# State-space heads: a select in place of four subtractions, one product for M, and an output projection cut into halves and quarters

## The chip, the cores and the metric

The kernel runs on one core of a Trainium2 chip, as one launch. The metric is device time in microseconds (us). Engines are named as in the profile: PE is TensorE (PEld its weight load), DVE is VectorE, ACT is ScalarE, POOL is GpSimd, SP issues most DMAs.

## The reference, cut to what matters

Six stages follow each other: a Mamba-2 mixer, three convolutional feed-forward blocks, a differential attention and a sparse-attention block. The change is in the first, the mixer, on 256 positions, 32 heads of 64 channels, two chunks of 128 positions:

```python
zxbcdt = rms_norm(x, ln_g) @ in_w                 # z, xs, B, C, dt
xbc = silu(causal_dwconv(xbc, conv_w, conv_b))
dt = softplus(dt + dt_bias); a = dt * (-exp(a_log))
a_cs = cumsum(a) within a chunk                   # per head
decay_in = exp(where(l >= s, a_cs[l] - a_cs[s], -inf))
y_diag = einsum('bcgls,bgrcls,bcsgrp->bclgrp', C B^T, decay_in, xs * dt)
y_off  = (state that enters chunk 1) read by C, times exp(a_cs)
y = (y_diag + y_off + xs * d_skip) * silu(z)
y = rms_norm(y in 4 groups of 512 channels) * norm_g
x = x + y @ out_w                                 # 2048 -> 1024
```

With two chunks, everything between source and target positions is three blocks of 128 by 128 for a head: chunk 0 to itself, chunk 1 to itself, and chunk 0 to chunk 1. Each is a product M of a decay block E and a block CB of C and B; y is xd (xs times dt) times M.

## The kernel before

Every large product is split in three: an operand is a high and a low part (fp32r), and hi*hi, hi*lo and lo*hi are summed in PSUM. A piece of weights is 128 x 1024 (eight blocks of 128 rows for one output tile of 128 columns) and makes 24 matmuls of 128x256. `split` makes a piece: ACT copies the raw weights to `wh` (L257), then `wl = raw - wh` is done by DVE (L261) or, where the step number is in `POOLED`, by POOL (L259). Five pieces may be ready ahead (`NS = 5`), and `cap` lowers that.

The mixer projects dt, then 8 tiles of B and C, 16 tiles of xs, and 16 tiles of z; then 8 output tiles of 16 blocks (two pieces) each. While the z tiles run, the heads are worked on in a pipeline of eight stages, two heads (one tile t of 128 channels) at a time. After each tile (`step`) one unit of the pipeline is recorded: s7 of tile t-7, s6 of t-6, and so on down to s0 of t. There are 23 units for 16 z tiles; the rest run beside the first output tiles.

- s0 loads `abc`, the cumulative sums of two heads along the free axis, the same in all partitions (a DMA issued on ACT's queue).
- s1 makes E: on DVE four `tensor_scalar` (L724, L726: subtract the partition's own sum, then min with 0), on ACT the exponentials; PE transposes xs (L733).
- s2 makes xd (L739) and M: two products on DVE for the blocks on the diagonal (L745), one on POOL for the third (L746). CB holds zeros above the diagonal.
- s3: six matmuls (L757), read by s4 on DVE (L763).
- s5 multiplies by z on POOL (L777), squares on ACT (L778) and adds squares on POOL (L781).
- s6, for every fourth t: sums of squares over channels on PE (L463), then scale (DVE, L302) and power -1/2 (POOL, L303). s7: a broadcast on PE (L476), a product on DVE (L795), high parts on ACT (L796) and low parts on POOL or DVE (L797); these are the operands of the output projection.
- `zpost`: tanh on ACT and a product on DVE (L771).

A scheduler turns the recorded program into one queue per engine; it orders by its own costs. Each engine then works its queue strictly in order. The output projection's first halves (blocks 0 to 7) of `AHEAD = 3` tiles stand behind the z tiles; then the remaining units are recorded, then the second halves of these tiles and the five others. PSUM has three buffers `mm` for large products and five `ax` for the rest.

Of the kernel before, what the change touches and what calls it, by code (L numbers as in the profile page):

```python
# [10 lines left out]
F32 = mybir.dt.float32  # L11
# [12 lines left out]
NEG = -1e30  # L24
# [154 lines left out]
class Net:  # L179
# [425 lines left out]
    def mamba(self, pool, nxt):  # L605
# [9 lines left out]
        acs = tl("acs", [128, 3, 32])  # L615
        scr = self.dr.tile([32, 256], F32, name="acs_scr")
        BC = tl("BC", [128, 8, T])
        CB = tl("CB", [128, 4, 3, 128])

        def post_dt(pt):  # L620
# [32 lines left out]
            nc.gpsimd.dma_start(scr, at)  # L653
            self.out("dt", dt)
# [22 lines left out]
        def make_cb(g):  # L677
            p = self.ax()
            Bg, Cg = BC[:, g, :], BC[:, 4 + g, :]
            nc.tensor.matmul(p[:, 0:256], Bg[:, 0:128], Cg, start=True, stop=True)  # L680
            nc.tensor.matmul(p[:, 256:384], Bg[:, 128:256], Cg[:, 128:256], start=True, stop=True)
            pv = p[:, 0:384].rearrange("p (b l) -> p b l", b=3)
            nc.vector.tensor_tensor(CB[:, g, 0:3:2, :], pv[:, 0:3:2, :],
                                    U[:, None, :].to_broadcast([128, 2, 128]), op=ALU.mult)
            nc.scalar.activation(CB[:, g, 1, :], pv[:, 1, :], AF.Copy)

# [26 lines left out]
        def s0(t):  # L713
            a = tl("abc", [128, 2, T], 3)
            nc.scalar.dma_start(a, bass.AP(tensor=scr.tensor, offset=scr.offset + 512 * t,
                                           ap=[[0, 128], [256, 2], [1, 256]]))
            ABC[t] = a

        def s1(t):
            a = ABC.pop(t)  # L720
            e = tl("E", [128, 2, 3, 128], 2)
            for h in range(2):
                H = 2 * t + h
                nc.vector.tensor_scalar(e[:, h, 0, :], a[:, h, 0:128], acs[:, 0, H:H + 1], 0.0,  # L724
                                        op0=ALU.subtract, op1=ALU.min)
                nc.vector.tensor_scalar(e[:, h, 2, :], a[:, h, 128:256], acs[:, 1, H:H + 1], 0.0,  # L726
                                        op0=ALU.subtract, op1=ALU.min)
                self.act(e[:, h, 1, :], a[:, h, 128:256], AF.Exp, bias=acs[:, 2, H:H + 1])
            for b in (0, 2):
                self.act(e[:, :, b, :], e[:, :, b, :], AF.Exp)  # L730
            p = self.ax()
            for c in range(2):
                nc.tensor.transpose(p[:, c * 128:c * 128 + 128], xs[:, t, c * 128:c * 128 + 128], ident)  # L733
            E[t] = (e, p)

        def s2(t):
# [6 lines left out]
            mv = m.rearrange("p h (b l) -> p h b l", b=3)  # L743
            for h in range(2):
                nc.vector.tensor_tensor(mv[:, h, 0:3:2], e[:, h, 0:3:2, :], CB[:, t // 4, 0:3:2, :], op=ALU.mult)  # L745
            nc.gpsimd.tensor_tensor(mv[:, :, 1], e[:, :, 1, :], CB[:, t // 4, 1:2, :].to_broadcast([128, 2, 128]),  # L746
                                    op=ALU.mult)
            M[t], XD[t] = m, xd

        def s3(t):  # L750
            m, xd = M.pop(t), XD.pop(t)
            p = self.ax()

            for b in range(3):
# [857 lines left out]
```

## Time and profile before

| | |
|---|---|
| median of 3 runs | 1158.45 us (1158.36 to 1159.26) |
| profiled execution | 1157.68 us, its span 1155.9 us |
| PE busy | 1111.2 us, 96% |
| DVE busy | 946.9 us, 82% |
| ACT busy | 712.6 us, 62% |
| POOL busy | 178.3 us, 15% |
| mean granted PE clock | 0.986 of full |

A busy time includes the time for which an instruction that has begun is held up; so an instruction much longer than its like was waiting inside. Starts of instructions that follow each other on an engine with no idle time give the engine's real cost of one, which is below the duration shown, as neighbours overlap.

### The profile page before, as it was taken

How to read it: one execution, taken by the hardware profiler on the slowest of the kernel's cores; microseconds unless marked ns; L12 is line 12 of the kernel's file. 1: busy time of each engine (PE TensorE's matmuls, PEld its weight loads, DVE VectorE, ACT ScalarE, POOL GpSimd, SP SyncE). 2: the span in 40 equal slices, each digit the busy share in tenths (PEclk: the TensorE clock that was granted, in tenths of full speed). 3: DMA queues.
4: the chain of work that ended last, by engine and by line, in shares of the span. 5: the costliest groups of instructions: out<-in, count | busy, mean ns of one | idle time of the engine just before them, and what ended most of it. 6: DMA issues, size and time to landing. Idle time of an engine off the chain costs nothing. (4 is left out here: it accounts for less than half of the span.)

```text
span 1155.9 us, 23508 instructions
## 1 busy us (share of the span) xinstructions
PE 1111.2 (96%) x9174; PEld 1084.1 (94%) x9174; DVE 946.9 (82%) x1884; ACT 712.6 (62%) x1322; POOL 178.3 (15%) x162
## 2 busy tenths in 40 slices
PE   6899988999999999999999999999999998999997
PEld 5799887999999999988999999999999998999997
DVE  5987998789888877787889988679988988999742
ACT  6568565566666556878666654555687556666541
POOL 3202665212000114222000001100000030000010
PEclk8899988999999999999999999999999999999999
DMA  8355542548555766653466668575564754666530
GB/s 310 139 183 187 169 138 101 183 163 316 188 184 178 273 221 232 203 199 128 137 213 205 216 227 282 200 238 174 204 207 141 276 196 145 213 239 228 190 115 37
DMA packets 50190, 224.80 MB, mean 194 GB/s; under 512 B 5744, under 2 KB 10496, under 8 KB 31136
## 3 DMA queue, kind: packets, MB, share of 16 engines
q1 hardware_dynamic: 41616, 211.53, 52.8%
q10 hardware_dynamic: 7056, 7.46, 2.2%
q0 software_dynamic: 1408, 4.32, 1.1%
q8 instruction: 72, 1.18, 0.4%
q14 instruction: 38, 0.31, 0.1%
HBM read 222.11 MB, written 4.25 MB: 196 GB/s over the span
## 5 line engine op out<-in xcount | busy, mean ns | idle before, releaser
L257 ACT ACTIVATE wh<-raw 128x1024 fp32r<-128x1024 f32 (+2 forms) x360 | 370.8, 1032 | 290.5 <-PE mm L389 255.6
L261 DVE TENSOR_TENSOR wl<-raw,wh 128x1024 fp32r<-128x1024 f32 (+1 forms) x351 | 419.7, 1198 | 97.1 <-ACT wh L257 94.9
L388 PE MATMUL mm<-xh,wh 128*128 128x256 f32 x1624 | 463.0, 286 | 3.2 <-DVE cv L667 1.7
L389 PE MATMUL mm<-xl,wh 128*128 128x256 f32 x1624 | 459.0, 283 | 5.0 <-DVE xl L482 4.8
L390 PE MATMUL mm<-xh,wl 128*128 128x256 f32 x1624 | 458.6, 283 | 0.0
L388 PEld LDWEIGHTS mm<-xh,wh 128*128 128x128 f32 x1624 | 306.8, 189 | 7.6 <-issue 3.8
L389 PEld LDWEIGHTS mm<-xl,wh 128*128 128x128 f32 x1624 | 306.8, 189 | 6.1 <-DVE xl L482 5.5
L390 PEld LDWEIGHTS mm<-xh,wl 128*128 128x128 f32 x1624 | 306.7, 189 | 0.3 <-DVE sco L1172 0.3
L455 POOL TENSOR_TENSOR sqacc<-sqacc,sq 128x256 f32<-128x256 f32 x42 | 50.7, 1207 | 649.9 <-issue 395.4
L388 PE MATMUL mm<-hh,wh 128*128 128x256 f32 x528 | 147.7, 280 | 0.0
L389 PE MATMUL mm<-hl,wh 128*128 128x256 f32 x528 | 147.5, 279 | 0.0
L390 PE MATMUL mm<-hh,wl 128*128 128x256 f32 x528 | 147.2, 279 | 0.0
L860 DVE SCALAR_TENSOR_TENSOR cv<-mm,par,cv 128x255 f32<-128x255 f32 x240 | 114.3, 478 | 2.1 <-ACT cv L858 0.7
L389 PEld LDWEIGHTS mm<-hl,wh 128*128 128x128 f32 x528 | 99.2, 188 | 0.0
L390 PEld LDWEIGHTS mm<-hh,wl 128*128 128x128 f32 x528 | 99.2, 188 | 0.0
L388 PEld LDWEIGHTS mm<-hh,wh 128*128 128x128 f32 x528 | 99.2, 188 | 0.0
L586 DVE SCALAR_TENSOR_TENSOR ada<-ada,silu_c 128x512 f32<-128x512 f32 x96 | 67.0, 702 | 8.9 <-DMA ada<-in_wada_dram 8.8
L858 ACT ACTIVATE cv<-mm,par 128x256 f32<-128x256 f32 x120 | 65.7, 548 | 0.0
L388 PE MATMUL mm<-rw,wh 128*128 128x256 f32 (+2 forms) x168 | 50.7, 302 | 8.4 <-ACT wh L257 8.4
L389 PE MATMUL mm<-rw,wh 128*128 128x256 f32 (+2 forms) x168 | 50.2, 299 | 0.1
L390 PE MATMUL mm<-rw,wl 128*128 128x256 f32 (+2 forms) x168 | 50.0, 297 | 0.0
L388 PEld LDWEIGHTS mm<-rw,wh 128*128 128x128 f32 (+1 forms) x168 | 33.2, 198 | 8.7 <-ACT wh L257 8.4
(305 smaller groups left out, 1883.3 us busy)
## 6 DMA issues: line engine op xcount, KB each, us to landing
raw<-in_w_dram SPq DMA_DIRECT2D x148, 1024.0 KB, 4.9
ada<-in_wada_dram SPq DMA_DIRECT2D x96, 256.0 KB, 3.5
raw<-in_w_dram SPq DMA_DIRECT2D x23, 896.0 KB, 4.7
raw<-in_w_dram SPq DMA_DIRECT2D x6, 768.0 KB, 4.4
abc<-acs_scr ACTq DMA_DIRECT2D x16, 256.0 KB, 3.2
rel_bias_scr<-rel_bias_row POOLq DMA_DIRECT2D x8, 384.0 KB, 13.2
bias<-rel_bias_scr ACTq DMA_DIRECT2D x16, 128.0 KB, 2.9
x<-in_xT_dram SPq DMA_DIRECT2D x4, 256.0 KB, 4.2
```

What stands on the lines that cost most here:

```text
L257: nc.scalar.activation(wh[:, :n], src, AF.Copy)
L261: self.pace = nc.vector.tensor_tensor(wl[:, :n], src, wh[:, :n].bitcast(F32), op=ALU.subtract)
L388: nc.tensor.matmul(out, h, xh[:, k, :], start=first and a == 0, stop=False)
L389: nc.tensor.matmul(out, h, xl[:, k, :], start=False, stop=False)
L390: nc.tensor.matmul(out, l, xh[:, k, :], start=False, stop=last and a == n - 1)
L455: nc.gpsimd.tensor_tensor(self.acc, self.acc, s, op=ALU.add)
L586: i = nc.vector.scalar_tensor_tensor(t, t, 1.0, self.sc[:, h * 512:h * 512 + 512], op0=ALU.mult, op1=ALU.mult, accum_out=self.part[:, h, m ...
L858: nc.scalar.activation(c, pt, AF.Identity, scale=w(2), bias=P(cb, ct))
L860: nc.vector.scalar_tensor_tensor(c[:, d:], pt[:, :T - d], w(2 - d), c[:, d:], op0=ALU.mult, op1=ALU.add)
```

## The change

1. E. One `affine_select` on POOL (512 elements a partition) copies the two diagonal blocks of `abc` and puts -1e30 above the diagonal. The subtraction moves into the exponentials: six on ACT, 128x128 each, with the negated sums `nacs` as bias (a new small DVE instruction in `post_dt`), where there were two of 128x128 and two of 128x256. The four DVE `tensor_scalar` of a tile go.
2. M. One product on DVE of 768 elements takes the place of two of 256 on DVE and one of 256 on POOL. E and CB are laid out with the two diagonal blocks first, and s3 takes the blocks in another order.
3. `POOLED` loses 22, 26, 30, 34, 38 and 42: these `wl` are made on DVE.
4. From the z tiles to the third output tile, PE's queue is kept in the order of the program.
5. First halves of five output tiles instead of three stand behind the z tiles, two of them in `ax` buffers. Then three pieces are taken, and their blocks 8 to 11 (quarters) run, one pipeline unit after each of the first two; blocks 12 to 15 of the three tiles follow, block by block. While this lasts `cap` is 2.
6. The scratch of the cumulative sums has another layout, so that the same 256 KB load brings chunk by chunk.

```diff
-AHEAD = 3
+AHEAD, HELD = 5, 3
-POOLED = {"mamba": (1, 3, 5, *range(22, 44, 4))}
+POOLED = {"mamba": (1, 3, 5)}
...
+            nc.vector.tensor_scalar(nacs.rearrange("p c h -> p (c h)"), p[:, 0:64], -1.0, None, op0=ALU.mult)
...
         def s1(t):
             a = ABC.pop(t)
-            e = tl("E", [128, 2, 3, 128], 2)
+            e = tl("E", [128, 3, 2, 128], 2)
+
+            nc.gpsimd.affine_select(e[:, 0:2].rearrange("p c h l -> p (c h) l"), a.rearrange("p c h l -> p (c h) l"),
+                                    [[0, 4], [1, 128]], ALU.is_ge, NEG, base=0, channel_multiplier=-1)
             for h in range(2):
                 H = 2 * t + h
-                nc.vector.tensor_scalar(e[:, h, 0, :], a[:, h, 0:128], acs[:, 0, H:H + 1], 0.0,
-                                        op0=ALU.subtract, op1=ALU.min)
-                nc.vector.tensor_scalar(e[:, h, 2, :], a[:, h, 128:256], acs[:, 1, H:H + 1], 0.0,
-                                        op0=ALU.subtract, op1=ALU.min)
-                self.act(e[:, h, 1, :], a[:, h, 128:256], AF.Exp, bias=acs[:, 2, H:H + 1])
-            for b in (0, 2):
-                self.act(e[:, :, b, :], e[:, :, b, :], AF.Exp)
+                self.act(e[:, 2, h, :], a[:, 1, h, :], AF.Exp, bias=acs[:, 2, H:H + 1])
+                for c in range(2):
+                    self.act(e[:, c, h, :], e[:, c, h, :], AF.Exp, bias=nacs[:, c, H:H + 1])
...
-            for h in range(2):
-                nc.vector.tensor_tensor(mv[:, h, 0:3:2], e[:, h, 0:3:2, :], CB[:, t // 4, 0:3:2, :], op=ALU.mult)
-            nc.gpsimd.tensor_tensor(mv[:, :, 1], e[:, :, 1, :], CB[:, t // 4, 1:2, :].to_broadcast([128, 2, 128]),
-                                    op=ALU.mult)
+            nc.vector.tensor_tensor(mv, e.rearrange("p b h l -> p h b l"),
+                                    CB[:, t // 4, None].to_broadcast([128, 2, 3, 128]), op=ALU.mult)
...
-        pts = [self.tileB_f("ssm_out_w", 0, 8, 16, yH, yL) for m in range(AHEAD)]
-        self.flush()
-        self.drain()
-        self.out("y", xs)
-        nxt()
-        for m in range(8):
+        with self.tc.manual_schedule(engines={mybir.EngineType.PE}):
+            for t in range(16):
+                self.tileB("ssm_in_w", 8, xh, xl, zpost(t))
+            pts = []
+            for m in range(AHEAD):
+                pt = (self.ps() if m < HELD else self.ax())[:, 0:T]
+                pts.append(self.tileB_f("ssm_out_w", 0, 8, 16, yH, yL, pt=pt))
+
+            self.cap = self.NS - HELD
+            ws = []
+            for m in range(HELD):
+                ws.append(self.piece("ssm_out_w"))
+                for k in range(8, 12):
+                    self.mm_f(pts[m], ws[m], k, yH, yL)
+                self.step()
+            self.flush()
+            self.drain()
+            self.out("y", xs)
+            nxt()
+            for k in range(12, 16):
+                for m in range(HELD):
+                    self.mm_f(pts[m], ws[m], k, yH, yL)
+            self.cap = self.NS
+            for m in range(HELD):
+                self.later(1, lambda m=m: self.add_x(m, pts[m]))
+            self.step()
+        for m in range(HELD, 8):
...
+    def mm_f(self, pt, w, k, fh, fl):
+
+        nc = self.nc
+        c = slice(k % 8 * 128, k % 8 * 128 + 128)
+        nc.tensor.matmul(pt, w[0][:, c], fh(k), start=k == 0, stop=False)
+        nc.tensor.matmul(pt, w[0][:, c], fl(k), start=False, stop=False)
+        nc.tensor.matmul(pt, w[1][:, c], fh(k), start=False, stop=k == 15)
```

How the queues are filled shows at two places. The first is DVE's queue amid the z tiles, before; M_1765 is the M of tile 7, E_1847 the E of tile 9, rs_1750 the first group's scale, rw the tile xs:

```order
L763 SCALAR_TENSOR_TENSOR rw_609<-rw_609,par_81,ax_1684 128x256
L771 SCALAR_TENSOR_TENSOR z_1674<-z_1674,mm_1649 128x256
L739 TENSOR_TENSOR xd_1763<-ax_1706,dt_189 128x256
...
L726 TENSOR_SCALAR E_1769<-abc_1709,acs_190 128x128
L745 TENSOR_TENSOR M_1765<-E_1697,CB_193 128x2x128 x2
L724 TENSOR_SCALAR E_1847<-abc_1781,acs_190 128x128
L726 TENSOR_SCALAR E_1847<-abc_1781,acs_190 128x128
L724 TENSOR_SCALAR E_1847<-abc_1781,acs_190 128x128
L302 TENSOR_SCALAR rs_1750<-ax_1745 128x2
```

The same place in the changed program; M_1692 is the M of tile 6, M_1763 that of tile 7, rs_1748 the same group's scale:

```order
L761 SCALAR_TENSOR_TENSOR rw_611<-rw_611,par_81,ax_1683 128x256
L745 TENSOR_TENSOR M_1692<-E_1633,CB_194 128x768
L740 TENSOR_TENSOR xd_1761<-ax_1704,dt_189 128x256
L769 SCALAR_TENSOR_TENSOR z_1673<-z_1673,mm_1648 128x256
L261 TENSOR_TENSOR wl_1677<-raw_1272,wh_1676 128x1024
L302 TENSOR_SCALAR rs_1748<-ax_1743 128x2
L761 SCALAR_TENSOR_TENSOR rw_611<-rw_611,par_81,ax_1754 128x256
```

Between s4 of tile 5 and the group's scale DVE's queue held z, xd, four subtractions of tile 8, two products of tile 7 and three subtractions of tile 9; now it holds one M, one xd, one z and one `wl`.

The second place is PE's queue behind the last s3 (L757, L755). Before; mm_2203, mm_2260 and mm_2315 are the three output tiles, z_1951 and z_2163 squares of the last group, rs_2383 its scale:

```order
L757 MATMUL ax_2365<-M_2311,xd_2309 64x128 x6
L463 MATMUL ax_2378<-onec_86,z_1951 128x1 x2
L830 MATMUL mm_2203<-xh0_2347,wh_2088 128x256
L830 MATMUL mm_2260<-xh0_2347,wh_2166 128x256
...
L463 MATMUL ax_2378<-onec_86,z_2163 128x1 x2
L832 MATMUL mm_2203<-xh0_2347,wl_2089 128x256
L831 MATMUL mm_2260<-xl0_2348,wh_2166 128x256
L832 MATMUL mm_2260<-xh0_2347,wl_2167 128x256
L830 MATMUL mm_2260<-xh0_2347,wh_2166 128x256
L476 MATMUL ax_2386<-con_82,rs_2383 128x128 x2
```

In the changed program (here 24 matmuls each of ax_2360 and ax_2395, the fourth and fifth tile's first halves, and 12 of mm_2194, come between the last s3 and the sums; where rows of one piece follow, the first stands):

```order
L843 MATMUL mm_2194<-xh0_2335,wh_2219 128x256
...
L463 MATMUL ax_2438<-onec_86,z_1946 128x1 x2
L463 MATMUL ax_2438<-onec_86,z_2155 128x1 x2
L843 MATMUL mm_2250<-xh0_2335,wh_2275 128x256
...
L476 MATMUL ax_2458<-con_82,rs_2443 128x128 x2
L843 MATMUL mm_2303<-xh0_2335,wh_2328 128x256
...
L843 MATMUL mm_2194<-xh0_2335,wh_2219 128x256
```

Before, four matmuls stood between the last sums and the broadcast that needs them; now there are 12, and 12 more behind it. From the first z tile to the last s3, PE's queue has the same order in both programs, except for one pair of transposes that stood inside an s3.

## Rows read from the trace of the kernel before

**Rows 1.** Timeline of PE; start, us, instruction, in brackets idle time and releaser.

```profile
113.33 0.88 PE L757 MATMUL ax<-M,xd 128*64 128x128 f32 x12
...
117.38 0.88 PE L757 MATMUL ax<-M,xd 128*64 128x128 f32 x12
...
139.97 1.11 PE L757 MATMUL ax<-M,xd 128*64 128x128 f32 x12
...
147.84 1.22 PE L476 MATMUL ax<-con,rs 128*128 128x128 f32 x4 [3.52 <-POOL rs L303]
...
154.86 0.88 PE L757 MATMUL ax<-M,xd 128*64 128x128 f32 x12
...
162.83 0.95 PE L463 MATMUL ax<-onec,z 128*128 128x1 f32 x8
...
167.66 0.61 PE L476 MATMUL ax<-con,rs 128*128 128x128 f32 x4
...
172.25 1.07 PE L757 MATMUL ax<-M,xd 128*64 128x128 f32 x12
...
180.59 0.66 PE L757 MATMUL ax<-M,xd 128*64 128x128 f32 x2 [2.69 <-DVE M L745]
...
193.04 0.88 PE L757 MATMUL ax<-M,xd 128*64 128x128 f32 x12
...
207.16 0.28 PE L830 MATMUL mm<-yh,wh 128*128 128x256 f32 x1
...
212.81 0.28 PE L830 MATMUL mm<-yh,wh 128*128 128x256 f32 x1
```

**Rows 2.** Two stretches: length, busy per engine (count), PEclk, DMA share, GB/s.

```profile
144.00:154.00 10.00, 6.48 (x39) 5.72 (x38) 9.91 (x22) 6.69 (x17) 7.41 (x9) 0.66 0.42 146
178.00:188.00 10.00, 7.41 (x40) 6.56 (x40) 10.00 (x20) 4.37 (x12) 6.78 (x6) 0.66 0.30 106
```

**Rows 3.** Timeline of DVE amid the z tiles, and once much later.

```profile
115.34 0.41 DVE L745 TENSOR_TENSOR M<-E,CB 128x256 f32<-128x256 f32 x1
115.68 0.27 DVE L726 TENSOR_SCALAR E<-abc,acs 128x128 f32<-128x128 f32 x1
115.87 1.22 DVE L261 TENSOR_TENSOR wl<-raw,wh 128x1024 fp32r<-128x1024 f32 x1
...
120.03 2.40 DVE L724 TENSOR_SCALAR E<-abc,acs 128x128 f32<-128x128 f32 x1
...
126.54 0.47 DVE L763 SCALAR_TENSOR_TENSOR rw<-rw,par,ax 128x256 f32<-128x256 f32 x1
126.93 0.41 DVE L771 SCALAR_TENSOR_TENSOR z<-z,mm 128x256 f32<-128x256 f32 x1
127.26 0.41 DVE L739 TENSOR_TENSOR xd<-ax,dt 128x256 f32<-128x256 f32 x1
...
803.78 1.22 DVE L261 TENSOR_TENSOR wl<-raw,wh 128x1024 fp32r<-128x1024 f32 x1
```

**Rows 4.** Groups of DVE, 105 to 210 us: busy us, mean ns of one.

```profile
L745 DVE TENSOR_TENSOR M<-E,CB 128x256 f32<-128x256 f32 x32 | 21.1, 683 | 0.5 <-ACT E L294 0.5
L724 DVE TENSOR_SCALAR E<-abc,acs 128x128 f32<-128x128 f32 x28 | 14.2, 509 | 0.2
```

**Rows 5.** Timeline of POOL amid the z tiles, and twice much later.

```profile
118.42 0.74 POOL L777 TENSOR_TENSOR rw<-rw,z 128x256 f32<-128x256 f32 x1 [0.74 <-DVE rw L763]
119.81 2.53 POOL L259 TENSOR_TENSOR wl<-raw,wh 128x1024 fp32r<-128x1024 f32 x1 [0.65 <-ACT wh L257]
...
803.55 1.61 POOL L1178 TENSOR_SCALAR_AFFINE_SELECT sco<-sco 128x128 f32<-128x128 f32 x1 [28.70 <-DVE sco L1174]
...
808.86 0.39 POOL L1179 TENSOR_SCALAR_AFFINE_SELECT sco<-sco 128x256 f32<-128x256 f32 x1 [2.90 <-DVE sco L1174]
```

**Rows 6.** Groups of ACT, 105 to 210 us.

```profile
L257 ACT ACTIVATE wh<-raw 128x1024 fp32r<-128x1024 f32 x22 | 23.0, 1050 | 4.3 <-PE mm L831 2.9 <-PE mm L389 1.4
L294 ACT ACTIVATE E<-abc,acs 128x128 f32<-128x128 f32 x32 | 10.9, 390 | 2.5 <-issue 2.5
```

More of the change, by code (lines that the diff above doesn't have):

```diff
@@ L615, in mamba @@
         acs = tl("acs", [128, 3, 32])
-        scr = self.dr.tile([32, 256], F32, name="acs_scr")
+        nacs = tl("nacs", [128, 2, 32])
+        scr = self.dr.tile([2, 32, 128], F32, name="acs_scr")
         BC = tl("BC", [128, 8, T])
@@ L650, in post_dt @@
             nc.vector.tensor_copy(acs.rearrange("p c h -> p (c h)"), p[:, 0:96])
+            nc.vector.tensor_scalar(nacs.rearrange("p c h -> p (c h)"), p[:, 0:64], -1.0, None, op0=ALU.mult)
             at = tl("acsT", [32, T])
             nc.vector.tensor_copy(at, p2[0:32, 0:T])
-            nc.gpsimd.dma_start(scr, at)
+            nc.gpsimd.dma_start(scr.rearrange("c h l -> h c l"), at.rearrange("h (c l) -> h c l", c=2))
             self.out("dt", dt)
@@ L682, in make_cb @@
             pv = p[:, 0:384].rearrange("p (b l) -> p b l", b=3)
-            nc.vector.tensor_tensor(CB[:, g, 0:3:2, :], pv[:, 0:3:2, :],
+            nc.vector.tensor_tensor(CB[:, g, 0:2, :], pv[:, 0:3:2, :],
                                     U[:, None, :].to_broadcast([128, 2, 128]), op=ALU.mult)
-            nc.scalar.activation(CB[:, g, 1, :], pv[:, 1, :], AF.Copy)
+            nc.scalar.activation(CB[:, g, 2, :], pv[:, 1, :], AF.Copy)
         for t in range(8):
@@ L713, in s0 @@
         def s0(t):
-            a = tl("abc", [128, 2, T], 3)
-            nc.scalar.dma_start(a, bass.AP(tensor=scr.tensor, offset=scr.offset + 512 * t,
-                                           ap=[[0, 128], [256, 2], [1, 256]]))
+            a = tl("abc", [128, 2, 2, 128], 3)
+            nc.scalar.dma_start(a.rearrange("p c h l -> p c (h l)"), bass.AP(tensor=scr.tensor, offset=scr.offset + 256 * t,
+                                           ap=[[0, 128], [4096, 2], [1, 256]]))
             ABC[t] = a
@@ L752, in s3 @@
             p = self.ax()
-            for b in range(3):
-                oc = slice(min(b, 1) * 128, min(b, 1) * 128 + 128)
+            for b, c, oc in ((0, 0, slice(0, 128)), (2, 0, slice(128, 256)), (1, 1, slice(128, 256))):
                 for h in range(2):
-                    nc.tensor.matmul(p[64 * h:64 * h + 64, oc], xd[:, b // 2, h, :], m[:, h, b * 128:b * 128 + 128],
-                                     start=b < 2, stop=b != 1)
+                    nc.tensor.matmul(p[64 * h:64 * h + 64, oc], xd[:, c, h, :], m[:, h, b * 128:b * 128 + 128],
+                                     start=b != 1, stop=b != 2)
             YP[t] = p
@@ L802, in mamba @@
         self.pipe(16, [s0, s1, s2, s3, s4, s5, s6, s7])
-        for t in range(16):
-            self.tileB("ssm_in_w", 8, xh, xl, zpost(t))
         yH = lambda k: yt(k)[0]
         yL = lambda k: yt(k)[1]
-        pts = [self.tileB_f("ssm_out_w", 0, 8, 16, yH, yL) for m in range(AHEAD)]
-        self.flush()
-        self.drain()
-        self.out("y", xs)
-        nxt()
-        for m in range(8):
+        with self.tc.manual_schedule(engines={mybir.EngineType.PE}):
[24 more added lines that the diff above has]
+        for m in range(HELD, 8):
             self.out_tile(m)
```

## The prediction

> **What bounds the kernel now.** I read the shares first: PE is busy for 96% of the span, so a change can only win where PE waits or runs at its lower clock. The part that the change touches is the z tiles with their heads and the output projection behind them, about 101 to 236 us; every queue behind it is in the same order in both programs. There I read PE's timeline [rows 1]. A full step (one z tile of 24 matmuls, one s3, one pair of transposes) takes 117.38 - 113.33 = 4.05 us when nothing is late. The sums of a group (L463) cost 0.95 and its broadcast (L476) 0.61, an s3 0.88, and in the regular end 48 matmuls take 212.81 - 207.16 = 5.65, so 24 take 2.82. With these the stretches compare with what PE needed in them:
>
> - 113.33 to 139.97: 6 steps and the sums, 25.25; took 26.64; lost 1.4.
> - 139.97 to 154.86: 2 steps and a broadcast, 8.7; took 14.89; lost 6.2.
> - 154.86 to 172.25: 4 steps, sums, broadcast, 17.8; took 17.4; nothing lost.
> - 172.25 to 193.04: 2 steps, a half tile, sums, broadcast, s3: 8.1 + 2.82 + 0.95 + 0.61 + 0.88 = 13.4; took 20.8; lost 7.4.
> - 193.04 to 207.16: s3, sums, broadcast and 72 matmuls, 0.88 + 0.95 + 0.61 + 8.47 = 10.9; took 14.1; lost 3.2.
>
> Together 18.2 us: 15.0 while heads are worked on (call it A) and 3.2 at the pipeline's end (B). In A, PE stood idle for 3.52 us on the scale of a group and for 2.69 us on an M [rows 1]; around both the granted clock falls to a mean of 0.66, so part of these stretches ran at the 1.2 GHz level instead of 2.4, after the idle time [rows 2]. In both, DVE is busy for 9.91 and 10.00 of 10 us [rows 2]: DVE is late, and PE pays.
>
> Why DVE is late: by starts [rows 3], a subtraction costs 0.19, a product of 256 0.34, s4 0.39, the z product 0.33, `wl` 1.14; xd is like z's product, s7's product like s4, its low part like a product of 256. For one tile: 4 x 0.19 + 2 x 0.34 + 0.39 + 0.33 + 0.33 + 12/16 x 1.14 (four of 16 z-stage pieces are made on POOL) + 0.39 + half of 0.34 = 3.9 us. PE's pace is 4.05 + (0.95 + 0.61)/4 = 4.44. So DVE would keep up but for waits inside its instructions: the product's mean is 683 ns where an undisturbed one shows 410, the subtraction's 509 against 270 [rows 3, 4]. That is 2 x 0.27 + 4 x 0.24 = 1.5 us a tile, 5.4 in all. What holds them: the subtraction at 120.03 lasts 2.40 us, just while POOL makes a `wl` (119.81, 2.53 us) [rows 3, 5]. (5.4 - 4.44) x 15 tiles = 14 us of backlog, close to A's 15.0.
>
> **The change part by part.**
>
> *E and M on DVE.* The four subtractions go (0.76 us a tile). M of 768: from 256 to 1024 elements DVE's time rises from 0.34 to 1.14, 1.04 ns an element, so 0.34 + 512 x 0.00104 = 0.87, against 0.68. All `wl` are now DVE's: +0.29 a tile. Sum: 0.87 + 0.39 + 0.33 + 0.33 + 1.14 + 0.39 + 0.17 = 3.6 us. DVE's own work falls only by 0.3 us a tile; what matters is the waits. The subtractions, which waited for 0.96 us of the 1.5, are gone, and so are POOL's 2.5 us instructions behind which they waited. The trace shows no M of 768 and no `wl` beside a select, so I bound the waits: below 0 (none held up), above the 1.5 of now. Nearest is the old product's 0.27 for one instruction; with M, `wl` and half a low part that is 2.5 x 0.27 = 0.7. DVE then needs 4.3 against PE's 4.44 and keeps up. With 1.5 it needs 5.1.
>
> The select on POOL: 128 x 256 took 0.39; 128 x 128 took 1.61, but there a `wl` on DVE had begun at 803.78 and was through, at 1.14 a piece, at 804.92, so the select worked only for the last 0.24 [rows 3, 5]. The step of 0.15 for 128 elements gives 0.39 + 0.30 = 0.69 for 512. POOL has this, s5's 0.74, half of another such for the squares and half for the low parts: 2.2 us a tile, of 4.44. Bounds for one select: 0.39 and 0.39 + 0.74.
>
> ACT: six exponentials of 390 ns [rows 6] in place of two such and two wider ones; they overlap, start to start about 0.3, so 1.8 us in place of 1.2. With `wh` (1.05), tanh, square and high part about 3.8 us of 4.44: covered by the z tile. If that cover went, it would cost 0.6 a tile.
>
> The chain of one M: s4 of an older tile, s5, select, exponentials, M: 0.4 + 0.74 + 0.69 + 1.8 + 0.87 = 4.5 us, for which there are two steps, 8.1. The DMA that loads `abc` stands on ACT's queue right behind the exponentials of the tile before and is hidden by the tanh and `wh` behind it only in part; the two steps hold that as well.
>
> What stays in A: after each broadcast s7's burst stands in DVE's queue, four products and two low parts, 4 x 0.39 + 0.68 = 2.2 us ahead of the next s4; against the spare time the M behind it comes about 0.5 late, twice: 1.0. Chance waits of 0.15 a step on 13 steps, 2.0. The first M, which now waits for six exponentials behind a table load, 0.3. A falls from 15.0 to 3.3: **-11.7**. With waits at the upper bound it keeps (5.1 - 4.44) x 15 = 9.9; with none, 0.
>
> *PE in the program's order.* From the first z tile to the last s3 the queue already had that order, so here this is worth nothing. It matters only at the end.
>
> *The end.* Behind the last s3 PE now has 48 matmuls of two more first halves and 12 of a quarter (7.1 us) before the sums, while s4, s5 and the square need 0.4 + 0.74 + 0.4 and two `wl`. Then 12 (1.4 us) before the broadcast, while DVE's scale and POOL's power need about 1.1 if the `wl` ahead of the scale is done. Then 12 more (1.4) while the first s7 product, its high part and POOL's low part take 0.4 + 0.4 + 0.74 with their handovers, 1.8: 0.4 late. I leave 0.4 for this and 0.6 for the scale: B falls from 3.2 to 1.0, **-2.2**; bounds 0 and -3.2. Holding three pieces leaves two buffers; the pieces for the fourth and fifth tile's second halves are ready in them, 5.6 us, in which the next one is split (1.05 + 1.14): hidden. The three sums into x come together on DVE, 3 x 0.41, beside those 5.6 us: hidden. `nacs`, and the write of the sums in smaller pieces, come 60 us before the first use: hidden, otherwise 0.2 once.
>
> Sum against the profiled execution: 1157.7 - 11.7 - 2.2 = 1143.8. The median shown is 0.77 above that execution: 1144.5.
>
> **The rivals.**
>
> *DVE stays late (1).* Its own work is nearly unchanged, 3.9 against 3.6, and M is now one long instruction that POOL can hold up or that holds up POOL. For it: the 9.91 and 10.00 of 10 us; against it: the waits that I can see are mostly subtractions behind POOL's `wl`. Then A keeps 9.9: 1157.7 - 5.1 - 2.2 = 1150.4, and 1151.2 by the median's measure.
> The Trainium skill, GPSIMD Engine Reference, section Specifications, says that GpSimd's SBUF interfaces are shared with VectorE and collide with instructions in a two-port mode or with two SBUF inputs. The trace agrees for the subtraction (2.40 us beside POOL's `wl`) and for the products' 683 ns. By that rule M and `wl`, with two SBUF inputs each, keep colliding with every POOL instruction, which is this rival.
>
> *Only the end gains (2).* If something else paces the heads, say the load of `abc`, select and six exponentials in line (the load is not in my 4.5), A stays and B gains: 1156.3. Against it: PE's two long waits name DVE's M and a scale that stood behind DVE's queue.
>
> *POOL becomes the pace: slower (3).* Every select now stands before its M, and POOL takes its instructions in order. If each of its three for a tile waits out a DVE instruction as the select at 803.55 did (1.61 - 0.24 = 1.37), POOL needs 2.2 + 4.1 = 6.3 us a tile against the 5.4 of now: 15 x 0.9 - 2.2 = 11 us slower, 1169. It decides from a wait of (5.4 - 2.2)/3 = 1.1 for each. Against it: s5 at 118.42 shows 0.74, hence no wait.
>
> **How the numbers follow.** Forecast 0.62, rival 1 0.21, rival 2 0.08, rival 3 0.05, and 0.04 for no change through two effects that cancel. The predicted time is the forecast's, 1144.5. Its own range is 1140.3 (A and B both gone: 1158.45 - 18.2) to 1148. The range of 8 in 10 takes in rival 1 for the most part: 1140 to 1151.5. What a measurement can tell from no change is about 0.2%, 2.3 us: faster 0.89 (forecast, rival 1, part of rival 2), the same 0.05, slower 0.06.
>
> **What would show it.** Right: steps of 4.05 to 4.3 us from s3 to s3 to the end of the z tiles, no granted clock below full in that stretch, DVE with some idle time, M at 0.9 to 1.3 us, the select at 0.7, and no PE wait over 1 us before the regular end, which begins some 14 us earlier. Wrong on A: M or `wl` at twice their time with DVE still full (rival 1), ACT waiting on POOL's select and M on ACT (rivals 2 and 3). Wrong on B: PE idle at the last broadcast, or at the first low part behind it. Wrong altogether: a select of several us.

## The result and the profile after

The changed kernel takes 1145.84 us (median of 5 runs, 1144.22 to 1147.73) where the kernel before takes 1158.45 (median of 5, 1157.59 to 1159.26); the ratio is 0.9891, 95% interval 0.9876 to 0.9906. The forecast was 1144.5, in a range of 1140 to 1151.5. The profiled execution of the changed kernel is its slowest, 1147.73 us with a span of 1146.0.

Two landmarks show where the time went: the first s3 amid the z tiles, and the first scale (L302, DVE) of the norm behind the mixer. Before, they stand at 113.33 [rows 1] and 240.0 us, 126.7 apart; now at 113.23 and 228.5, 115.2 apart. So 11.4 us were gained in the stretch of which the prediction speaks. The spans differ by only 9.9, because PE's lower clock shows up in later stages, whose queues are in the same order, twice after (at 540 and 765 us) and once before (at 953 us), for 1.7 us each. I call the distance of the two landmarks S and use it for all runs below, since it is free of that. S comes from one execution of each kernel, and a stretch of lower clock can come in one execution and not in the next: the five runs of e7 below lie between 1145.09 and 1151.06 us, at mean granted clocks of 0.994 and 0.987. So a difference of 2 us in S is a strong sign only where the medians show it too.

The timeline of PE after (start, us, instruction, in brackets idle time and releaser), to be held against [rows 1]:

```profile
113.23 0.88 PE L755 MATMUL ax<-M,xd 128*64 128x128 f32 x12
117.28 0.88 PE L755 MATMUL ax<-M,xd 128*64 128x128 f32 x12
...
129.39 0.88 PE L755 MATMUL ax<-M,xd 128*64 128x128 f32 x12
134.88 0.88 PE L755 MATMUL ax<-M,xd 128*64 128x128 f32 x12 [1.37 <-DVE M L745]
...
145.08 0.88 PE L755 MATMUL ax<-M,xd 128*64 128x128 f32 x12 [0.82 <-DVE M L745]
...
155.11 0.88 PE L755 MATMUL ax<-M,xd 128*64 128x128 f32 x12 [1.88 <-DVE M L745]
...
160.31 0.60 PE L463 MATMUL ax<-onec,z 128*128 128x1 f32 x4 [0.77 <-ACT z L776]
...
174.28 0.88 PE L755 MATMUL ax<-M,xd 128*64 128x128 f32 x12 [0.87 <-DVE M L745]
...
179.22 0.61 PE L463 MATMUL ax<-onec,z 128*128 128x1 f32 x4 [0.51 <-ACT z L776]
...
184.02 0.88 PE L755 MATMUL ax<-M,xd 128*64 128x128 f32 x12
...
191.96 0.95 PE L463 MATMUL ax<-onec,z 128*128 128x1 f32 x8
...
194.38 0.71 PE L476 MATMUL ax<-con,rs 128*128 128x128 f32 x4
...
196.93 0.38 PE L844 MATMUL mm<-xl,wh 128*128 128x256 f32 x1 [0.29 <-POOL xl L795]
```

The last s3 comes at 184.02 instead of 193.04, so 8.9 of the 11.4 us are gained among the heads and 2.5 behind them. PE does not run in regular steps, though: it waits four times for M and twice for a square, 6.2 us in all. Before, the waits that the same view shows among the heads were the 3.52 on the group's scale, 3.0 on M and 0.4 on a low part, 6.9 in all, hardly more.

What is gone on PE's side is the lower clock. Stretches after, and for comparison one of before in a later stage (length, busy per engine and count in the order PE, PEld, DVE, ACT, POOL, then PEclk, DMA share, GB/s):

```profile
150.00:160.00 10.00, 7.67 (x68) 7.24 (x68) 8.53 (x14) 6.60 (x18) 8.05 (x9) 1.00 0.57 180
174.00:184.00 10.00, 9.20 (x86) 8.69 (x86) 7.76 (x11) 7.47 (x18) 7.08 (x7) 1.00 0.31 107
540.00:550.00 10.00, 8.76 (x61) 8.55 (x60) 6.90 (x16) 5.13 (x10) 1.74 (x1) 0.83 0.31 107
765.00:775.00 10.00, 9.39 (x59) 8.37 (x58) 5.89 (x15) 3.71 (x6) 0.00 (x0) 0.83 0.53 183
```

```profile
953.00:963.00 10.00, 8.75 (x60) 8.54 (x60) 6.12 (x13) 5.10 (x13) 1.75 (x1) 0.83 0.32 105
```

What stood at 0.66 [rows 2] is at 1.00, with DVE at 8.53 and 7.76 of 10 us instead of 9.91 and 10.00. A stretch of 10 us at 0.83 costs 1.7 us, one at 0.66 costs 3.4. Summed over windows of 5 us from the first s3 on, (1 - PEclk) x 5 is 6.85 us before and 0.00 after. So the 11.4 us are 2.3 of listed waits (8.8 before, 6.5 after, the end included), 6.85 of lower clock, and 2.2 that neither view itemizes.

This is PE's account, and it doesn't say what set the pace. Before, DVE was busy for 77.73 of the 79.71 us from the first to the last s3 (the line is shown with e8). PE at its upper clock all the way could have shortened that stretch by no more than DVE's idle time, about 2 us. Now DVE is busy for 58.47 of 70.79 us.

What holds M up now: DVE groups after, 105 to 205 us (busy us, mean ns of one, idle time before them and its releasers):

```profile
L261 DVE TENSOR_TENSOR wl<-raw,wh 128x1024 fp32r<-128x1024 f32 x22 | 29.0, 1320 | 3.0 <-ACT wh L257 3.0
L745 DVE TENSOR_TENSOR M<-E,CB 128x768 f32<-128x768 f32 x16 | 17.3, 1082 | 10.7 <-POOL rw L775 5.5 <-POOL E L725 2.9 <-ACT E L294 1.9
```

DVE stands idle for 10.7 us before M's, where it had 0.5 us before the products of [rows 4]. It is no longer late; it waits for the chain in front of it, the load of `abc`, the select on POOL, the exponentials on ACT.

### The profile page after: what moved, and what is told of

It is laid out like the page before. It is cut to its first block, busy times and chain, and to the rows that moved or that the text cites. A ratio compares the mean times of both kernels' runs of the same rounds, so it can differ in the third digit from the quotient of the medians.

```text
span 1146.0 us, 23469 instructions
## 1 busy us (share of the span) xinstructions
PE 1103.4 (96%) x9174; PEld 1079.1 (94%) x9174; DVE 929.8 (81%) x1811; ACT 718.2 (63%) x1354; POOL 161.9 (14%) x156
## 5 line engine op out<-in xcount | busy, mean ns | idle before, releaser
L261 DVE TENSOR_TENSOR wl<-raw,wh 128x1024 fp32r<-128x1024 f32 (+1 forms) x357 | 428.0, 1201 | 94.1 <-ACT wh L257 91.8
L455 POOL TENSOR_TENSOR sqacc<-sqacc,sq 128x256 f32<-128x256 f32 x42 | 48.4, 1153 | 646.6 <-issue 395.7
L886 DVE SCALAR_TENSOR_TENSOR cv<-mm,par,cv 128x255 f32<-128x255 f32 x240 | 114.4, 478 | 2.1 <-ACT cv L884 0.7
L451 ACT ACTIVATE sq<-x 128x256 f32<-128x256 f32 x49 | 19.9, 409 | 35.7 <-DVE x L522 21.3
## 6 DMA issues: line engine op xcount, KB each, us to landing
rel_bias_scr<-rel_bias_row POOLq DMA_DIRECT2D x8, 384.0 KB, 11.5
```

Of the source, the lines that this page charges most:

```text
L261: self.pace = nc.vector.tensor_tensor(wl[:, :n], src, wh[:, :n].bitcast(F32), op=ALU.subtract)
L451: nc.scalar.activation(s, self.x[:, k, :], AF.Square)
L455: nc.gpsimd.tensor_tensor(self.acc, self.acc, s, op=ALU.add)
L886: nc.vector.scalar_tensor_tensor(c[:, d:], pt[:, :T - d], w(2 - d), c[:, d:], op0=ALU.mult, op1=ALU.add)
```

## The experiments

Medians are each with the ratio to the kernel before on the same chip. S is of the profiled execution; "waits" is the sum of what the view of PE's waits lists between the two landmarks, "clock" is the sum of (1 - PEclk) x 5 us there. Line numbers shift by a few in some of these kernels.

| kernel | median us | ratio (95%) | S | waits | clock |
|---|---|---|---|---|---|
| before | 1158.45 | 1 | 126.7 | 8.8 | 6.85 |
| changed | 1145.84 | 0.9891 (0.9876 to 0.9906) | 115.2 | 6.5 | 0 |
| e1 before, new end | 1155.37 | 0.9974 (0.9964 to 0.9984) | 123.1 | 7.7 | 5.15 |
| e3 before, no late `wl` on POOL | 1156.93 | 0.9992 (0.9980 to 1.0004) | 126.2 | 8.4 | 5.15 |
| e10 before, one M | 1155.76 | 0.9980 (0.9970 to 0.9989) | 123.2 | 10.3 | 3.40 |
| e5 changed, `wl` back on POOL | 1147.87 | 0.9914 (0.9899 to 0.9929) | 115.8 | 5.6 | 1.70 |
| e8 changed, subtractions back | 1146.24 | 0.9911 (0.9881 to 0.9941) | 114.4 | 6.2 | 0 |
| e6 changed, third block on POOL | 1151.95 | 0.9962 (0.9948 to 0.9975) | 121.7 | 7.7 | 5.10 |
| e13 changed, three M on DVE | 1152.11 | 0.9946 (0.9925 to 0.9967) | 122.3 | 7.5 | 5.15 |
| e7 changed, scheduler orders PE | 1149.64 | 0.9937 (0.9915 to 0.9959) | 117.8 | 6.4 | 1.70 |
| e4 changed, other scratch | 1142.77 | 0.9876 (0.9860 to 0.9892) | 112.5 | 3.9 | 0 |
| e9 e4, low parts on DVE | 1147.71 | 0.9921 (0.9898 to 0.9943) | 115.8 | 4.6 | 3.40 |
| e12 e4, low parts behind s4 | 1145.01 | 0.9880 (0.9863 to 0.9896) | 115.1 | 3.6 | 3.40 |
| e14 e4, select ahead of the sum | 1140.96 | 0.9871 (0.9852 to 0.9891) | 110.1 | 1.9 | 0 |

**e1, the end alone.** In the kernel before: `AHEAD, HELD = 5, 3`, and the block under `manual_schedule` in place of the old end.

> The kernel before with only the changed end (five first halves, quarters of three tiles, PE in program order); subtractions, three products and the pieces on POOL stay. Theory (two separate gains, A among the heads and B at the end): only B comes, 3.2 us of PE waits at the end fall to about 0.5, so 2.7 us faster, 1155.7; the first scale of the norm behind the mixer comes at 237.3 instead of 240.0; the two waits of 3.5 and 2.7 us among the heads stay. Rival (only the end gains): nearly the whole 12.6 us, under 1148. Second rival (the two gains are tied, the end can't gain while DVE is late): 1158.4, no change.

Measured: 0.26% faster (0.16 to 0.36), 3.0 us; the norm's scale at 236.5. The waits of 3.5 us on the scale and 2.7 on M stay, and so does a full DVE (77.60 of 78.87 us from the first to the last s3). The end's gain is its own, a little above the 2.2 predicted; the rival that the whole gain is here is out.

**e3, only the late `wl` off POOL, in the kernel before.**

```diff
-POOLED = {"mamba": (1, 3, 5, *range(22, 44, 4))}
+POOLED = {"mamba": (1, 3, 5)}
```

> The kernel before with only the six late pieces wl moved from POOL to DVE. Theory (the subtractions are held up inside by POOL's 2.5 us wl): the subtraction's mean falls from 0.50 to under 0.35 us, DVE's need falls although its own work grows by 0.29 us a tile, and half or more of A's 15.0 us goes: 1150 (1147 to 1153). Rival (DVE's own work sets the backlog): 0.29 us on 16 tiles more, 4.6 us slower, 1163; the subtractions stay at 0.5 us because s5, the products and the squares on POOL hold them as well.

Measured: not told from no change. The half of the theory on the subtractions holds, as DVE's group between 105 and 205 us shows:

```profile
L724 DVE TENSOR_SCALAR E<-abc,acs 128x128 f32<-128x128 f32 x28 | 9.8, 351 | 0.1
```

Their mean falls from 509 ns [rows 4] to 351. In that window the 56 subtractions save 8.5 us, the six `wl` more add 6.0 (18.8 to 24.8 us in that group), the products 1.2. From the first to the last s3, the same work for PE in every kernel, something does come of it (length, busy per engine as above):

```profile
113.09:187.80 74.71, 69.26 (x605) 62.43 (x604) 73.41 (x157) 47.48 (x109) 39.49 (x42) 0.98 0.46 152
```

DVE is busy 4.3 us less (73.41 for 77.73), and the heads take 5.0 us less (74.71 for 79.71). Behind the last s3 4.5 of these are lost again (51.5 us to the norm's scale for 47.0): there the old end now shows 3.4 us of lower clock and 3.4 of waits, for none and 1.9 before. So the subtractions were held up as read and freeing them helps the heads; by the median the kernel gains nothing of it.

**e8, the subtractions back, in the changed kernel.**

```diff
-            nc.gpsimd.affine_select(e[:, 0:2].rearrange("p c h l -> p (c h) l"), a.rearrange("p c h l -> p (c h) l"),
-                                    [[0, 4], [1, 128]], ALU.is_ge, NEG, base=0, channel_multiplier=-1)
...
+                for c in range(2):
+                    nc.vector.tensor_scalar(e[:, c, h, :], a[:, c, h, :], acs[:, c, H:H + 1], 0.0,
+                                            op0=ALU.subtract, op1=ALU.min)
...
+            for c in range(2):
+                self.act(e[:, c], e[:, c], AF.Exp)
```

> The changed kernel with the four subtractions of a tile on DVE and the two wide exponentials again, no select; one product for M and no wl on POOL stay. Theory (the subtractions are what made DVE late): DVE needs 3.6 + 4 x 0.19 = 4.4 us of its own work and 0.7 to 1.2 of waits a tile against PE's 4.44, so a backlog of 0.6 to 1.1 us a tile comes back: 8 to 11 us slower, 1154 to 1157; the norm's first scale at 236.5 to 239. Rival (one product for M and no wl on POOL carry the gain): under 3 us slower, 1148.5, scale under 231.5.

Measured: not told from the changed kernel; S is 114.4, 0.9 below. Both theory and rival had allowed for some loss. The stretch from the first to the last s3, of before, of the changed kernel and of this one:

```profile
113.33:193.04 79.71, 72.62 (x605) 65.84 (x604) 77.73 (x154) 47.13 (x111) 52.85 (x49) 0.91 0.44 141
```

```profile
113.23:184.02 70.79, 64.57 (x605) 60.05 (x604) 58.47 (x89) 53.43 (x142) 41.11 (x43) 1.00 0.51 159
```

```profile
112.71:182.80 70.09, 64.26 (x605) 59.81 (x605) 69.47 (x144) 46.25 (x109) 25.08 (x29) 1.00 0.54 162
```

DVE is busy for 77.73 of 79.71 us before and for 69.47 of 70.09 here: full in both, so that in both its time is the length of the stretch, and here it needs 8.3 us less although the subtractions are back. They are no longer held up (group of DVE, 105 to 205 us):

```profile
L728 DVE TENSOR_SCALAR E<-abc,acs 128x128 f32<-128x128 f32 x56 | 14.5, 316 | 0.0
```

Before, the 56 took 28.0 us. So the waits that the prediction saw were real, and they go when POOL's `wl` and its share in M go (POOL busy for 25.08 us, for 52.85 before); the subtractions need not leave DVE for that. With the select DVE has 12 us to spare, and in the changed kernel this buys nothing.

**e5, the `wl` back on POOL, in the changed kernel.** The diff of e3, reversed.

> The changed kernel with the six late pieces wl on POOL again, 2.5 us each. Theory (POOL's wl holds up whatever DVE has beside it): M and the wl beside them last 1 to 2 us longer and select and s5 stand behind 2.5 us in POOL's queue, PE waits 4 to 8 us more: 1150 to 1154. Rival (only the subtractions were held up, and they are gone): DVE is freed of 6 x 1.14 us, no loss or up to 2 us gained, 1144 to 1146.

Measured: S 0.5 longer, with one stretch of lower clock (1.7 us); the ratio is 0.0023 higher (2.7 us), with intervals that overlap. It lies between the two theories: in the changed kernel, where DVE has room (53.79 us busy of 70.36), the move is worth little, 0.5 us by S.

**e6, M by three products again, and e13, the same with all three on DVE.** e13 differs from e6 in the engine of the last product alone:

```diff
-            nc.vector.tensor_tensor(mv, e.rearrange("p b h l -> p h b l"),
-                                    CB[:, t // 4, None].to_broadcast([128, 2, 3, 128]), op=ALU.mult)
+            for h in range(2):
+                nc.vector.tensor_tensor(mv[:, h, 0:2], e[:, 0:2, h, :], CB[:, t // 4, 0:2, :], op=ALU.mult)
+            nc.vector.tensor_tensor(mv[:, :, 2], e[:, 2, :, :], CB[:, t // 4, 2:3, :].to_broadcast([128, 2, 128]),
+                                    op=ALU.mult)
```

> The changed kernel with M made by three products again: two of 256 on DVE, the third block's on POOL. Theory (what the heads gain comes from taking work and the waits that go with it off DVE and POOL together): POOL gets some 0.75 to 1 us a tile more, which collides with DVE's instructions beside it; DVE's own work falls only by 0.2 us a tile; PE waits 2 to 4 us more, 1148 to 1150, the norm's first scale at 230.5 to 232.5 instead of 228.5. Rival (M is not what counts, POOL has room, and a shorter M on DVE is earlier): 1145.8 or less, scale at 228.5 or before.

> The changed kernel with M made by three products of 256, all on DVE. Theory (it is POOL's product that costs): DVE's own work rises by 3 x 0.34 - 0.88 = 0.14 us a tile, nothing stands behind it on POOL: at most 1.5 us slower than the changed kernel, 1146 to 1147.3; the norm's first scale at 228.5 to 230. Rival (one long instruction counts, since each shorter one can be held up once): like the run with the third block on POOL, 1150 to 1152, scale at 232 to 235.

Measured: S + 6.5 and + 7.0, e6 beyond what its theory gave, e13 as its rival said. So in the changed kernel it isn't POOL's share in M that counts; three products cost about the same on either engine. Groups of DVE in e13, 105 to 205 us:

```profile
L746 DVE TENSOR_TENSOR M<-E,CB 128x256 f32<-128x256 f32 x32 | 16.6, 522 | 9.0 <-ACT E L294 5.3 <-POOL rw L777 2.3 <-POOL E L725 1.3
L747 DVE TENSOR_TENSOR M<-E,CB 128x256 f32<-128x256 f32 x16 | 8.1, 504 | 0.0
```

That is 24.7 us for what one product does in 17.3, 0.46 us a tile. DVE isn't full by it (62.85 us busy of 78.05 from the first to the last s3; 56.52 of 77.51 in e6), so its load isn't what costs here. PE's waits in the table grow by only 1.2 and 1.0 us; where they fall and what the clock then does makes the difference. PE in e13, and its stretches:

```profile
162.02 0.82 PE L463 MATMUL ax<-onec,z 128*128 128x1 f32 x4 [2.14 <-ACT z L778]
...
183.05 1.01 PE L463 MATMUL ax<-onec,z 128*128 128x1 f32 x4 [1.94 <-ACT z L778]
```

```profile
160.00:170.00 10.00, 7.98 (x64) 7.34 (x65) 7.90 (x17) 8.91 (x24) 4.08 (x6) 0.83 0.50 164
180.00:190.00 10.00, 8.06 (x50) 7.63 (x49) 6.01 (x10) 7.83 (x18) 5.55 (x7) 0.66 0.41 121
```

The sums now wait for squares, and behind both waits the clock is at its lower level for a part of the stretch. ACT shows why the square is late:

```profile
158.87 0.70 ACT L294 ACTIVATE E<-E,nacs 128x128 f32<-128x128 f32 x2 [3.72 <-POOL E L725]
...
161.56 0.40 ACT L778 ACTIVATE z<-rw 128x256 f32<-128x256 f32 x1
```

The exponentials wait 3.72 us for the select, and the square stands behind them in ACT's queue. On POOL that select (158.21) stood behind an addition of squares (156.53, 1.72 us), which stood behind an s5, which had waited for DVE's s4. POOL's queue has the same order there in the changed kernel, so what is later is what comes through it.

**e10, one M alone, in the kernel before.**

```diff
-            for h in range(2):
-                nc.vector.tensor_tensor(mv[:, h, 0:3:2], e[:, h, 0:3:2, :], CB[:, t // 4, 0:3:2, :], op=ALU.mult)
-            nc.gpsimd.tensor_tensor(mv[:, :, 1], e[:, :, 1, :], CB[:, t // 4, 1:2, :].to_broadcast([128, 2, 128]),
-                                    op=ALU.mult)
+            nc.vector.tensor_tensor(mv, e, CB[:, t // 4, None].to_broadcast([128, 2, 3, 128]), op=ALU.mult)
```

> The kernel before with one edit: M is one product of 768 on DVE (two on DVE and one on POOL before). Subtractions on DVE, six wl on POOL, the old end and PE's order by the scheduler stay. Theory, revised after the runs that split M and brought the subtractions back (the third block's product on POOL is what made the heads late, by its wait for the exponentials in POOL's queue and by holding DVE): 6 to 8 us faster, 1150 to 1152; the norm's first scale at 232 to 234 instead of 240.0. Rival (my prediction's theory: the subtractions wait behind POOL's wl and stay where they are, DVE's own work rises by 0.2 us a tile): under 2 us faster, 1156.5 or more, scale after 238.

Measured: 2.5 us by the median, 0.20% (0.11 to 0.30), S - 3.5: between theory and rival. M lasts 1.26 us there and the L724 subtractions 0.55, beside POOL's `wl`. The stretch from the first to the last s3:

```profile
114.00:187.76 73.76, 66.17 (x605) 61.43 (x604) 73.44 (x140) 46.96 (x110) 37.53 (x32) 0.98 0.48 155
```

DVE is full again, with 4.3 us less to do, and the heads are 6.0 us shorter; 2.5 of these are lost behind the last s3. So before the change one M, or POOL free of its `wl`, each saves DVE about the same.

**e7, no order kept for PE.** The line `with self.tc.manual_schedule(...)` goes, its block stays.

> The changed kernel without the rule that keeps PE in program order. The scheduler then puts several of the s3 and the sums behind up to 14 matmuls of the next tile, and the s7 products partly ahead of an M. Theory (as predicted, the order is worth nothing among the heads and the end keeps its cover): within 1 us, 1145 to 1146.8, the norm's first scale at 228 to 229.5. Rival (the later s3 gives M the time that it lacks): PE's 4.9 us of waits on M fall by half, 2 us faster, 1143.5. Second rival (a later s3 makes s4, s5 and the sums later, and the end pays): 2 to 3 us slower, 1148.5.

Measured: S + 2.5, slower than the theory (its ratio's interval and the changed kernel's don't overlap), as the second rival says in size. The norm's scale comes at 231.4 instead of 228.5. The later s3 gave M nothing: PE waits 5.9 us for it, not less, and one wait of 1.76 us is followed by 1.7 us of lower clock.

**e4, the scratch laid out tile by tile,** in the changed kernel.

```diff
-        scr = self.dr.tile([2, 32, 128], F32, name="acs_scr")
+        scr = self.dr.tile([16, 2, 2, 128], F32, name="acs_scr")
...
-                                           ap=[[0, 128], [4096, 2], [1, 256]]))
+                                           ap=[[0, 128], [1, 512]]))
```

> The changed kernel with the scratch of the cumulative sums laid out tile by tile, so that a load of abc is one run of 2 KB for a partition instead of two of 1 KB. Theory (what is left among the heads is in part the load of abc, which lands in 4.9 us in the changed kernel against 3.3 before, since its packets have doubled from 1872 to 3536 in the stretch): landing comes back to 3.3, the waits of PE on M of 1.4 and 0.8 us go and the one of 1.9 falls, 2 to 3 us faster than the changed kernel: 1143.3; the norm's first scale at 226 instead of 228.5. Rival (the load is late because it shares the engines with the 1 MB loads of weights, or what is late is DVE behind the s7 products): landing stays above 4.5 or the waits stay, 1145.8.

Measured: S 112.5, 2.7 us less than the changed kernel; the ratio's interval reaches lower and overlaps. The DMA view from 100 to 200 us (queue: packets, MB, share; issue: count, KB, median us to landing), of before, the changed kernel and this one:

```profile
q10 hardware_dynamic: 1872, 3.41, 11.4%
...
abc<-acs_scr ACTq DMA_DIRECT2D x13, 256.0 KB, 3.3
```

```profile
q10 hardware_dynamic: 3536, 3.41, 14.9%
...
abc<-acs_scr ACTq DMA_DIRECT2D x13, 256.0 KB, 4.9
```

```profile
q10 hardware_dynamic: 1872, 3.41, 11.5%
...
abc<-acs_scr ACTq DMA_DIRECT2D x13, 256.0 KB, 3.4
```

The same bytes in twice the packets land 1.6 us later. With one run of 2 KB the load is as quick as before the change, and PE's waits on M fall from 4.9 to 2.3 us.

**e9 and e12, the low parts of s7,** on top of e4. e9 gives all of them to DVE; e12 puts those of the first three groups on DVE behind the s4 that follows.

> The kernel with the scratch laid out tile by tile, and now all four low parts of an s7 on DVE (two were on POOL). Theory (two low parts on DVE beside two on POOL hold each other: 0.87 us each there against 0.34 undisturbed): four on DVE take 1.4 us instead of 1.75 for two, POOL's adds and products come 1.8 us sooner, the waits on M behind the s7 products (0.8 and 0.9 us) and on the squares (0.8 and 0.5) shrink by half; at the end the first low part is no longer waited for: 1 to 2 us faster than the scratch's own run, 1141.3; the norm's first scale at 225.2 instead of 226.5. Rival (DVE is the late one there, and two low parts more make it later): 0.5 to 1 us slower, 1143.5, scale at 227.2.

> The kernel with the scratch laid out tile by tile, the low parts of the first three groups all on DVE and put behind the s4 that follows the s7 products in DVE's queue (in the run with all low parts on DVE they stood ahead of it, and the squares of the next tiles came late). Theory (what is left is s4 standing behind the low parts): the waits of 0.8 and 0.9 us on M and of 0.8 and 0.5 us on the squares fall by half or more, 1.5 to 2 us faster than the scratch's own run, 1141; the norm's first scale at 224.8 instead of 226.5. Rival (any low part more on DVE makes M later, or the squares still come late through POOL): 1143.5 to 1147, scale at 227 to 229.

Measured: both theories miss; e9 is slower than its rival too, e12 came as its rival said. The waits on M fall (2.3 to 0.8 and 1.5 us), but the sums wait longer for a square, 2.06 and 1.76 us in e9, 1.84 in e12, so that the listed waits stay about where they were (3.9; 4.6 and 3.6). Each time the clock falls behind the wait for the square: 3.4 us in both profiled executions, and that is all of what S grows by (3.3 and 2.6). By the ratios e9 is slower than e4; e12 (0.9880) isn't told from it (0.9876).

**e14, the select ahead of the addition,** on top of e4. Three times the addition of two squares (then also L788) is recorded behind the select and kept there; all other queues are unchanged.

```diff
-                nc.gpsimd.tensor_tensor(z[b], z[b], z[t], op=ALU.add)
+                ADDS.append(t)
...
+                i = nc.gpsimd.tensor_tensor(z[b], z[b], z[t], op=ALU.add)
+                if sel is not None:
+                    self.after(i, sel)
```

> The kernel with the scratch laid out tile by tile, and one more edit: three times in POOL's queue the select of a tile now stands ahead of the addition of two squares instead of behind it; all other queues are the same. Theory (what still makes the sums late is the select on POOL: ACT stands idle for it, up to 4.0 us at 174.3, with six exponentials, a wh and the square that the sums need in line behind it): each of the three exponentials comes 1.3 to 1.7 us sooner, PE's waits on the squares (0.8 and 0.5) and the first one on M (0.6) go, the waits on M behind the s7 products (0.8 and 0.9) stay: 1.9 us faster than the scratch's own run, 1141; from the first s3 to the norm's first scale 110.7 us instead of 112.5. Rival (the addition, now later, puts s5 and so the squares as late as before, or the select meets DVE's wl there and lasts 1.6 us): no gain, 112.5 and 1142.8.

Measured: 1140.96 us, S 110.1, as the theory said. PE's waits from 112 to 226 us (us in total, times, longest; the middle one is in the norm, behind the second landmark):

```profile
PE ax L757 <- DVE M L747: 1.6, 2, 0.9
PE ax L476 <- POOL rs L303: 0.7, 1, 0.7
PE mm L855 <- POOL xl L806: 0.3, 1, 0.3
```

No sum waits for a square any more. The two waits left on M are those behind the s7 products, as expected. By S this version is 5.1 us ahead of the changed kernel and 2.4 ahead of e4; the ratios, 0.9871, 0.9891 and 0.9876, have intervals that overlap, so this gain rests on the profiled executions. From the first to the last s3 it takes 65.73 us. DVE with the subtractions would not fit into that: in e8 it needs 69.47. So the select may pay here after all; that is an estimate from these two, and no run tests it.

## Why the prediction was right, and where it was not

**The size.** Forecast -13.9 us in the stretch, measured -11.4: A -8.9 for -11.7, B -2.5 for -2.2 (e1 alone: 3.0 by the median).

**A, what bounded it.** The prediction took PE's loss for DVE's backlog: 5.4 us a tile against PE's 4.44. That step holds. Before, DVE needs 77.73 us for the 15 steps, 5.2 a tile, and is idle for 2.0; where it stays full, the heads take DVE's time (e3, e10, e8). Now it needs 3.9 (4.3 forecast) and has room. The lower clock, 6.85 us to none, was counted inside A without a term of its own; beside a full DVE it needed none, and it went with the long waits. In e6, e13 and e9 DVE isn't full, and there S grows by about what the lower clock takes (6.5 and 7.0 us for 5.1 and 5.15; 3.3 over e4 for 3.4).

**A, which part brings it.** "The subtractions, which waited for 0.96 us of the 1.5, are gone, and so are POOL's 2.5 us instructions behind which they waited" was the heart of the forecast. That step failed in its first half. With the subtractions back (e8) DVE's need falls to 4.6 us a tile all the same, and the kernel isn't told from the changed one. They are held up no longer because POOL lost its `wl` and its share in M. Each of these alone takes 4.3 us off DVE and 5.0 or 6.0 off the heads (e3, e10), of which the old end loses 4.5 and 2.5, so that by S 0.5 and 3.5 are left; what both together bring before the change, with the old end, no run shows. In the changed kernel, where DVE has room, the `wl` is worth 0.5 (e5) and one M in place of three 6.5 to 7.0 (e6, e13), by when things come and not by DVE's load. The prediction counted M as an added cost, 0.87 for 0.68 us. DVE's waits a tile were forecast at 0.7; M now stands 0.12 above its usual shortest (1.08 to 0.96), `wl` 0.10, half a low part 0.25: 0.5 together, so that term was good.

**Prices.** M by starts: 0.88 us for 0.87 forecast (112.08 to 112.96 on DVE). The select, 128x512, in POOL's timeline undisturbed and beside a `wl` of DVE:

```profile
141.50 0.63 POOL L725 TENSOR_SCALAR_AFFINE_SELECT E<-abc 128x512 f32<-128x512 f32 x1 [3.86 <-DMA abc<-acs_scr]
...
174.68 1.62 POOL L725 TENSOR_SCALAR_AFFINE_SELECT E<-abc 128x512 f32<-128x512 f32 x1
```

0.63 for 0.69, mean 0.97 of 14, inside the bounds of 0.39 and 1.13, so rival 3 never came near. POOL's need was forecast at 2.2 us a tile and is 2.7 (41.11 us for 15). Six exponentials of 390 ns: as forecast.

**Hidden, and not.** "The two steps hold that as well", on the load of `abc`: this failed. The new layout was written off as the same 256 KB; it made the load 1.6 us slower, and PE paid 2.7 by S (e4). "PE in the program's order is worth nothing among the heads" holds against the kernel before; against what the scheduler would do with the changed program it is worth 2.5 (e7).

**A, what is left.** Forecast 3.3 us: 1.0 for the s7 burst, 2.0 of chance, 0.3 for the first M. Measured 6.2: two waits on M behind the s7 products (1.88 and 0.87), two behind a late load (1.37 and 0.82), two on squares (0.77 and 0.51). The sign set for it, no wait over 1 us, failed twice. The sign for rival 2, ACT waiting on the select, showed: 9.1 us of idle time before the exponentials, without that rival's time. So the total came near although half of its heart was wrong, and that is in part luck: the subtractions, to which it gave the gain, left DVE together with the `wl` and the share in M whose leaving POOL did bring it. What it lacked, a late load and late squares, is 3.5 us of the waits left; the totals, A and B together, differ by 2.5. The chain of one M, 4.5 us with two steps for it, left out the load and what stands ahead of the select in POOL's queue: once DVE has room these hold up the heads, as the 2.7 and 2.4 us of S in e4 and e14 show.

**B.** Forecast 1.0 us left, measured 0.3: the sums and the broadcast come without a wait, the first low part with 0.29 for 0.4.

**The regular end** was to come some 14 us earlier; the norm behind it comes 11.5 earlier.

**Rival 1** by its rule: the Trainium skill, GPSIMD Engine Reference, section Specifications, has GpSimd and VectorE collide when a VectorE instruction has two SBUF inputs. The trace agrees that they do, and shows who pays more in this kernel: the select goes from 0.63 to 1.62 us beside a `wl`, while M's mean is 0.12 us above 0.96, though single ones last up to 1.42 and DVE's low parts 0.93 in the mean. DVE's need fell to 3.9 us a tile even so, and the rival's time did not come.

## What to carry to other kernels

Whether an engine sets the pace is read from its busy time over a stretch of the same work, in several versions: here the heads took DVE's time in each version in which DVE was full, and PE's 6.9 us of listed waits and 6.85 us of lower clock were what that looked like on PE. An engine that is held up can be relieved at the engine that holds it. Once it has room, relieving it more brings nothing by itself, and a repair that only moves a wait can lose: in e9 the wait moved from M to a square, and 3.4 us of lower clock came with it. Where several engines pass one tile along in order, ask for each queue what stands behind the instruction that waits; an addition of 1.7 us, put behind a select on an engine that is busy for 63% of the stretch (42.58 of 68.04 us in e4), was worth 2.4 us of S (e14). And a layout change has a price of its own: count the runs that a load makes of it, not its bytes.

## What was not expected of the hardware

- A load of 256 KB over 128 partitions as 256 runs of 1 KB landed in 4.9 us, as 128 runs of 2 KB in 3.4, beside the same loads of weights.
- The clock fell behind waits on PE of 1.84 (e12), 1.76 and 2.06 us (e9), all before the sums; it stayed at its upper level behind waits before an s3 of 1.88 (changed kernel) and 2.24 us (e8). But it fell behind waits before an s3 of 1.86 (e5) and 1.76 us (e7). What tells these apart stays open.
- 768 elements a partition in one DVE product took 1.08 us in the mean, in three of 256 on the same engine 1.54.
